# A scratch block in DRAM is turned around: the dense gates lie by group of four expert tiles, then partition, then block of 32 tokens

## The chip, the cores and the metric

The kernel runs on one core of a Trainium2 chip. The time is that of one execution on the device in microseconds (us). The kernel before took 4025.16 us, the median of three runs (4023.65 to 4027.57).

## The reference, cut to what matters

Two layers. Each has a mixer, and then a retrieval of experts ("PEER"): for every token, 8 heads pick 16 of 16,384 experts, each expert is one row of `U` and one of `V`, and the output is a gated sum.

```
q = (h @ w_q) per head and half;   s = q . subkeys
s_top, i_top = top_k(s, 16)                       # for both halves
best, pos = top_k(s_top[0] + s_top[1], 16)        # 16 of the 256 sums
idx = i_top[0][..] * 128 + i_top[1][..];  gate = softmax(best)
a   = einsum('td,thed->the', x, U[idx])
out = einsum('the,thed->td', gate * gelu(a), V[idx])
```

There are 544 tokens: 512 of a prompt and 32 of a sample group.

## The kernel before, in words

Of the 544 tokens the first 384 (`ND`) are computed densely: for every expert `a = gelu(x U^T)`, times a dense matrix of gates that is zero where an expert was not picked, times `V`. The other 160 tokens are done with gathered rows: indirect DMAs on POOL's queue fetch 128 rows of `U` or `V` at a time (tile `g_r`, four buffers), and DVE multiplies them out (`g_junk`, `g_acc`). The 16,384 experts are 128 tiles `j` of 128 partitions `i`; four tiles `j` are a group (`GA`), so there are 32 groups. The first 6 groups (`KEEP`) keep their activations in SBUF (tile `kept`), groups 6 to 17 write them to DRAM (`ad`, from tile `ga`, lines 934 and 941), and the rest are computed later, beside the dense sum.

The work of a layer around the change has two stages.

- **The gate stage.** For each of three blocks of 128 tokens, `second_stage` finds the picks and `make_g` builds the dense gates. For eight tokens at a time DVE writes one-hot matrices (`ohp`, `ohq`, `ohh`, `ohl`, lines 1360 to 1363), PE multiplies them (lines 1369 and 1370), and ACT copies the product into `stage` (line 1372), a tile of 128 partitions `i` by 128 tiles `j` by 32 tokens, in two buffers. After 32 tokens DVE multiplies the kept groups by their gates in place (line 1378), and ACT's queue writes the other 104 tiles `j` to the DRAM block `gd` (line 1379): 12 writes a layer, 24 in all. Expert activations (lines 95, 96, 115 and 934) and gathered rows are worked in between, by a budget of estimated times (`spend`).
- **The dense stage.** All 128 tiles `j` are taken in turn. For a group that isn't kept, SP's queue reads the group's gates from `gd` into `gt` (line 1079, two buffers), the activations `gr` come from `ad` or from `ga`, and DVE multiplies them (line 1092). Each is split into a high and a low part (`gwh` by ACT, `gwl` by DVE), `V` likewise (`vr` to `vh` and `vl`), and PE sums `gw^T v` for three blocks of tokens into PSUM (line 1113, 18 matmuls for a tile). The expert activations that are still missing (`wr` to `wh` and `wl`, then line 115) and the second half of the gathers run beside it.

The tiles of the dense stage (`gt`, `gwh`, `gwl`, `vr`) take the memory of the tiles of the gate stage (`stage`, the one-hot matrices). So the first to use such memory waits until the last reader of the old tile is done, and one of these readers is the last write of `gd`. The instructions of an engine run in the order in which they stand; a DMA queue takes its DMAs in the order in which they are issued, and a DMA's sixteen parts run on 16 DMA engines. In the profile, q1 is SP's queue, q10 ACT's, and q0 that of POOL's gathers.

Of the kernel before, what the change touches and what calls it, by code (L numbers as in the profile page):

```python
# [9 lines left out]
F32 = mybir.dt.float32  # L10
# [7 lines left out]
P = 128  # L18
# [17 lines left out]
NKEY = 128  # L36
# [8 lines left out]
ND = 384  # L45
# [3 lines left out]
ST = 32  # L49
TILE = (P, P, P, P, TS)  # L50
GA = 4
KEEP = 6
KJ = KEEP * GA
# [23 lines left out]
class Body:  # L77
# [881 lines left out]

    def peer(self, l):  # L960
        nc, a = self.nc, self.a
        gd = self.dp.tile([ND // ST, P, P, ST], F32, name=f"gd{l}")
        self.ad = self.dp.tile([P, NKEY // GA, GA, ND], F32, name=f"ad{l}")
        self.a_l, self.a_next, self.a_w = l, 0, None
        self.pre = {}
# [2 lines left out]
        with ExitStack() as es:  # L968
# [68 lines left out]
            with ExitStack() as es2:  # L1037
# [38 lines left out]
                for q in order:  # L1076
                    if q >= KEEP:
                        g4 = dn.tile([P, ND // ST, GA * ST], F32, name="gt", bufs=2)
                        nc.sync.dma_start(g4, gd[:, :, q * GA:(q + 1) * GA].rearrange("b i j t -> i b (j t)"))
                        if q < first // GA:  # L1080
                            ga4 = dn.tile([P, GA, ND], F32, name="gr", bufs=2)
                            nc.sync.dma_start(ga4, self.ad[:, q])
                        else:
                            ga4 = groups.pop(q)
                    for jj in range(GA):
                        j = q * GA + jj
# [33 lines left out]
                        if step % 4 == 0 and XAT <= step < XAT + 4 * (ND // P):  # L1120
                            i = (step - XAT) // 4
# [213 lines left out]
    def make_g(self, l, sp, gd, i, F):  # L1335

        nc = self.nc
        i1 = sp.tile([P, P], F16, name="i1T")
        i2 = sp.tile([P, P], F16, name="i2T")
        gh = sp.tile([P, P], F16, name="ghT")  # L1340
        gl = sp.tile([P, P], F16, name="glT")
        pr = self.bank(2)[:, :3 * P].rearrange("p (s t) -> p s t", s=3)
        for s in range(3):
            nc.tensor.transpose(pr[:, s], F[s].rearrange("p h k -> p (h k)"), self.ident)
        nc.scalar.copy(i1, pr[:, 0])
        nc.scalar.copy(i2, pr[:, 1])
        nc.scalar.activation(gh, pr[:, 2], AF.Copy, scale=GSCALE)
        nc.vector.scalar_tensor_tensor(gl, pr[:, 2], GSCALE, gh, op0=OP.mult, op1=OP.subtract)
        for c in range(0, P, OHT):
            if c % ST == 0:  # L1350
                stage = sp.tile([P, P, ST], F32, name="stage", bufs=2)

            sh = [P, OHT // 2, P, 2]

            def row(t):
                return t[:, c:c + OHT].rearrange("p (b t) -> p b t", t=2)[:, :, None, :].to_broadcast(sh)

            keys = self.io[:, None, :, :].to_broadcast(sh)
            p_, q_, qh, ql = (sp.tile(sh, F16, name=n, bufs=2) for n in ("ohp", "ohq", "ohh", "ohl"))
            nc.vector.tensor_tensor(p_, keys, row(i1), op=OP.is_equal)  # L1360
            nc.vector.tensor_tensor(q_, keys, row(i2), op=OP.is_equal)
            nc.vector.tensor_tensor(qh, q_, row(gh), op=OP.mult)
            nc.vector.tensor_tensor(ql, q_, row(gl), op=OP.mult)  # L1363
            self.spend(dve=2.45)
            for b in range(0, OHT, 4):
                ps = self.bank(2).rearrange("p (t j) -> p t j", t=4)
                for t in range(4):
                    w, half = (b + t) // 2, t % 2
                    nc.tensor.matmul(ps[:, t], p_[:, w, :, half], qh[:, w, :, half], start=True, stop=False)
                    nc.tensor.matmul(ps[:, t], p_[:, w, :, half], ql[:, w, :, half], start=False, stop=True)  # L1370
                o = (c + b) % ST
                nc.scalar.activation(stage[:, :, o:o + 4].rearrange("p j t -> p t j"), ps,  # L1372
                                     AF.Copy, scale=1.0 / GSCALE)
            self.t_pe += 0.9
            if (c + OHT) % ST == 0:
                t = i * P + c + OHT - ST
                k = self.kept[:, :, t:t + ST]
                nc.vector.tensor_mul(k, k, stage[:, :KJ])
                nc.scalar.dma_start(gd[t // ST, :, KJ:], stage[:, KJ:])

# [118 lines left out]
```

## Time and profile before

| | |
|---|---|
| median of three runs | 4025.16 us |
| the profiled execution's own time | 4027.84 us |
| its span | 4026.0 us |
| PE busy | 3878.3 us (96%) |
| DVE busy | 2950.2 us (73%) |
| ACT busy | 1603.4 us (40%) |
| POOL busy | 1038.8 us (26%) |
| granted clock of PE, mean | 0.978 |
| moved by DMA | 917.60 MB, mean 228 GB/s |

The profiled execution is 2.68 us longer than the median. Of its 4027.84 us, 1.84 us lie outside the span. The gate stage lies at about 980 to 1277 us in the first layer and 2960 to 3260 us in the second; the dense stage follows each. In the strips of 40 slices a slice is 100.65 us. Where a stage is judged, its own stretch of the trace is read, not the share over the span.

### The profile page before, as it was taken

What the parts mean: (1) busy time and instruction counts of PE and PEld (TensorE: products, weight loads), DVE (VectorE), ACT (ScalarE), POOL (GpSimd) and SP (SyncE); (2) the same over time, 40 slices, a digit from 0 to 9 for tenths busy, and PEclk for the clock granted to TensorE, in tenths of its full rate; (3) what the DMA queues carried; (4) which work ended last, traced back from release to release, by engine and by line L of the source; (5) the groups of instructions that cost most, each with busy time, mean ns of one, the idle gap of its engine ahead of it and who ended that gap; (6) DMA issues with size and microseconds to landing.
All of it is one profiled execution on the core that took longest, in us unless ns stands there. A gap on an engine that the chain in (4) does not pass through costs nothing.

```text
span 4026.0 us, 63148 instructions
## 1 busy us (share of the span) xinstructions
PE 3878.3 (96%) x24116; PEld 3522.3 (87%) x24116; DVE 2950.2 (73%) x5811; ACT 1603.4 (40%) x2373; POOL 1038.8 (26%) x880
## 2 busy tenths in 40 slices
PE   8999999999997999999999999999999889999998
PEld 7899997898996888888888999889989778888887
DVE  5544445789998888888855444467999978888887
ACT  4532333334554333333444333343355543333333
POOL 0110110003323444443401111000034434444443
PEclk9999999999997999999999999999999889999999
DMA  7233114427888999999933322162378899999996
GB/s 261 82 124 120 54 59 149 169 64 243 302 314 317 336 344 345 337 339 339 339 111 117 125 83 67 48 235 86 101 270 302 321 335 332 346 341 342 347 333 238
DMA packets 318272, 917.60 MB, mean 228 GB/s; under 512 B 28400, under 2 KB 109680, under 8 KB 314640
## 3 DMA queue, kind: packets, MB, share of 16 engines
q1 hardware_dynamic: 218896, 518.21, 38.0%
q0 software_dynamic: 92160, 335.59, 23.2%
q10 hardware_dynamic: 6912, 59.77, 3.7%
q8 instruction: 189, 3.10, 0.3%
q14 instruction: 115, 0.94, 0.1%
HBM read 826.19 MB, written 87.26 MB: 227 GB/s over the span
## 4 chain that ended last, share of the span: by engine, by line
PE 85%; DVE 8%; issue 3%; DMA 2%; ACT 2%; POOL 1%; DVEq 0%; POOLq 0%; SPq 0%; ACTq 0%
PE mm L115 31%; PE mm L1113 17%; PE sm L115 12%; PE sm L1113 9%; PE mm L341 2%; DVE wl L96 2%; DMA g_r<-u_rows,g_e 2%; DVE g_junk L1182 1%; PE sm L628 1%; PE sm L616 1%; PE sm L904 1%; PE sm L622 1%; PE sm L885 1%; DVE ohl L1363 1%; PE sm L522 1%
## 5 line engine op out<-in xcount | busy, mean ns | idle before, releaser
L95 ACT CAST wh<-wr 128x1024 fp32r<-128x1024 f32 (+1 forms) x464 | 466.9, 1006 | 1042.8 <-PE mm L115 676.0
L96 DVE TENSOR_TENSOR wl<-wr,wh 128x1024 fp32r<-128x1024 f32 (+1 forms) x464 | 543.3, 1171 | 384.2 <-ACT wh L95 383.5
L1197 POOL DMA_INDIRECT g_r<-u_rows,g_e x320 | 459.4, 1436 | 1374.3 <-DVE g_junk L1182 654.3
L1197 POOL DMA_INDIRECT g_r<-v,g_e x320 | 449.3, 1404 | 553.7 <-DVE g_acc L1190 511.1
L115 PE MATMUL mm<-ah,wh 128*128 128x384 f32 (+1 forms) x1408 | 467.5, 332 | 19.3 <-ACT ga L934 12.6
L115 PE MATMUL mm<-ah,wl 128*128 128x384 f32 (+1 forms) x1408 | 464.2, 332 | 15.0 <-DVE wl L96 14.7
L115 PE MATMUL mm<-al,wh 128*128 128x384 f32 (+1 forms) x1408 | 461.7, 328 | 0.5 <-DVE al L96 0.5
L1190 DVE SCALAR_TENSOR_TENSOR g_acc<-g_r,g_w,g_acc 128x1024 f32<-128x1024 f32 x320 | 409.7, 1280 | 12.3 <-DMA g_r<-v,g_e 10.3
L1182 DVE SCALAR_TENSOR_TENSOR g_junk<-g_r,h2t 128x1024 f16<-128x1024 f32 x320 | 390.0, 1219 | 30.3 <-DMA g_r<-u_rows,g_e 28.9
L96 DVE TENSOR_TENSOR vl<-vr,vh 128x1024 fp32r<-128x1024 f32 x256 | 312.3, 1221 | 38.7 <-ACT vh L95 38.3
L115 PE MATMUL mm<-hh,wh 128*128 128x272 f32 x1536 | 335.4, 295 | 0.2 <-ACT hh L95 0.2
L115 PE MATMUL mm<-hh,wl 128*128 128x272 f32 x1536 | 334.3, 295 | 0.0
L115 PE MATMUL mm<-hl,wh 128*128 128x272 f32 x1536 | 328.0, 293 | 0.0
L1113 PE MATMUL mm<-vl,gwh 128*128 128x512 f32 x1024 | 316.9, 390 | 0.0
L1113 PE MATMUL mm<-vh,gwl 128*128 128x512 f32 x1024 | 316.1, 390 | 0.0
L115 PE MATMUL sm<-ah,wl 128*128 128x384 f32 x896 | 303.5, 339 | 5.9 <-DVE wl L96 5.9
L1113 PE MATMUL mm<-vh,gwh 128*128 128x512 f32 x1024 | 304.1, 392 | 2.2 <-ACT vh L95 2.2
L115 PE MATMUL sm<-ah,wh 128*128 128x384 f32 x896 | 304.7, 340 | 0.7 <-ACT stage L1372 0.7
L115 PE MATMUL sm<-al,wh 128*128 128x384 f32 x896 | 303.6, 339 | 0.0
L115 PEld LDWEIGHTS mm<-ah,wh 128*128 128x128 f32 x1408 | 267.8, 190 | 28.2 <-ACT ga L934 18.8
L115 PEld LDWEIGHTS mm<-ah,wl 128*128 128x128 f32 x1408 | 267.6, 190 | 24.0 <-DVE wl L96 23.7
L95 ACT CAST vh<-vr 128x1024 fp32r<-128x1024 f32 x256 | 269.1, 1053 | 12.1 <-DMA vr<-v 11.4
(436 smaller groups left out, 8133.7 us busy)
## 6 DMA issues: line engine op xcount, KB each, us to landing
vr<-v SPq DMA_DIRECT2D x256, 512.0 KB, 6.9
wr<-u SPq DMA_DIRECT2D x240, 512.0 KB, 6.1
wr<-w_in SPq DMA_DIRECT2D x96, 512.0 KB, 3.6
gd<-stage ACTq DMA_DIRECT2D x24, 1664.0 KB, 8.5
gt<-gd SPq DMA_DIRECT2D x52, 768.0 KB, 10.7
ad<-ga ACTq DMA_DIRECT2D x24, 768.0 KB, 6.4
gr<-ad SPq DMA_DIRECT2D x24, 768.0 KB, 8.3
wr<-w_o SPq DMA_DIRECT2D x32, 512.0 KB, 3.8
```

The lines of the kernel that those rows point to most:

```text
L95: self.nc.scalar.copy(hi, src)
L96: self.nc.vector.tensor_sub(lo, src, hi.bitcast(F32))
L115: nc.tensor.matmul(o, w[:, k * P:(k + 1) * P], x[part][:, k], start=(q == 0), stop=(q == 3 * nk - 1))
L341: nc.tensor.matmul(ps[i][s][:np_], m[:, k, c], w[:, s * 512:(s + 1) * 512], start=(k == 0 and q == 0), stop=(k == NK - 1 and q == 2))
L522: nc.tensor.matmul(ps[i], x[:, k, i * P:(i + 1) * P], w[:, kk * BW:(kk + 1) * BW], start=(k == 0 and q == 0), stop=(k == NK - 1 and q == 2))
L616: nc.tensor.matmul(p[:, h], ats[:, h], dm[:, h], start=True, stop=True)
L622: nc.tensor.matmul(p[:, h], dtm[:, h], xm[:, h], start=True, stop=True)
L628: nc.tensor.matmul(p[:, h], xm[:, h], dtm[:, h], start=True, stop=True)
L1113: ins = nc.tensor.matmul(po[i][s], w[:, i * P:(i + 1) * P], v[:, s * 512:(s + 1) * 512], start=(step == 1 and m == 0), stop=(step == NKEY ...
L1182: ins = nc.vector.scalar_tensor_tensor(jk, r, 1.0, h2t[t], op0=OP.mult, op1=OP.mult, accum_out=w[:, s:s + 1])
L1190: nc.vector.scalar_tensor_tensor(acc[t], r, w[:, s:s + 1], acc[t], op0=OP.mult, op1=OP.add)
L1197: nc.gpsimd.indirect_dma_start(out=r, out_offset=None, in_=a["v" if which else "u_rows"].rearrange("l e d -> (l e) d"), in_offset=bass.Ind ...
```

## The change

The block `gd` of a layer had the axes block of 32 tokens, partition, tile `j`, token. Now it has group of four tiles, partition, block of 32 tokens, and then 128 elements (four tiles by 32 tokens). The bytes are the same, and so are the two DMA calls.

- The write (24 times, 1664 KB): a partition's 104 tiles by 32 tokens were one run of 13,312 bytes in DRAM, so the write was 128 runs. Now they are 26 runs of 512 bytes, 3328 runs in all. In SBUF they are contiguous in both.
- The read (52 times, 768 KB): a partition's gates of a group were 12 runs of 512 bytes, 1536 runs in all. Now they are one run of 6144 bytes, 128 runs in all.

```
-        gd = self.dp.tile([ND // ST, P, P, ST], F32, name=f"gd{l}")
+        gd = self.dp.tile([NKEY // GA, P, ND // ST, GA * ST], F32, name=f"gd{l}")
...
-                        nc.sync.dma_start(g4, gd[:, :, q * GA:(q + 1) * GA].rearrange("b i j t -> i b (j t)"))
+                        nc.sync.dma_start(g4, gd[q])
...
-                nc.scalar.dma_start(gd[t // ST, :, KJ:], stage[:, KJ:])
+                nc.scalar.dma_start(gd[KEEP:, :, t // ST].rearrange("q i j -> i q j"),
+                                    stage[:, KJ:].rearrange("p (q j) t -> p q (j t)", j=GA))
```

No instruction changes its place on any engine. These are the last rows of ACT's gate stage in the first layer, with the last write of `gd`:

```order
 L1372 ACTIVATE stage<-sm 128x4x128 x8
 L95 CAST wh<-wr 128x1024
-L1379 DMA gd_6639<-stage 128x3328
+L1379 DMA gd_6639<-stage 128x26x128
 L934 ACTIVATE ga<-sm 128x384
 L1187 ACTIVATE g_w_9072<-g_w_9072 128x16
```

The write stands between the same two instructions, and has 26 runs a partition in place of one. And this is SP's queue where the dense stage of the first layer begins:

```order
 L102 DMA wr<-u 128x1024 x32
 L1097 DMA vr<-v 128x1024 x3
-L1079 DMA gt<-gd_6639 128x12x128 x2
+L1079 DMA gt<-gd_6639 128x1536 x2
 L1082 DMA gr<-ad_6640 128x1536 x2
 L102 DMA wr<-u 128x1024 x3
```

Again only the shape differs: one run of 1536 elements a partition in place of 12 of 128.

## Rows read from the trace of the kernel before

**Rows 1.** The page: the DMA strip of 40 slices.
```profile
DMA  7233114427888999999933322162378899999996
```

**Rows 2.** Busy by stretch: length, PE, PEld, DVE, ACT, POOL, clock, DMA share, GB/s.
```profile
1000.00:1250.00 250.00, 224.12 (x1647) 210.84 (x1645) 248.47 (x377) 147.09 (x180) 79.40 (x54) 0.93 0.85 303
1300.00:1950.00 650.00, 648.90 (x3086) 565.34 (x3085) 535.74 (x648) 233.79 (x318) 280.56 (x206) 1.00 0.96 342
```

**Rows 3.** Waits of PE, 1290 to 2040 us: total us, times, longest.
```profile
PE mm L1113 <- ACT vh L95: 1.1, 1, 1.1
```

**Rows 4.** Chain of waits, 1150 to 1310 us: start, us, what.
```profile
1265.84 10.66 DMA gd<-stage
...
1277.70 14.33 PE sm L115 x72
```

**Rows 5.** Timeline of ACT, first layer: start, us, what, [idle before, releaser].
```profile
1232.20 0.33 ACTq L1379 DMA_DIRECT2D gd<-stage  x1
...
1247.28 0.33 ACTq L1379 DMA_DIRECT2D gd<-stage  x1
...
1265.84 0.33 ACTq L1379 DMA_DIRECT2D gd<-stage  x1
...
1276.92 0.51 ACT L95 CAST gwh<-kept 128x384 fp32r<-128x384 f32 x1 [5.85 <-DMA gd<-stage]
1277.34 1.04 ACT L95 CAST wh<-wr 128x1024 fp32r<-128x1024 f32 x1
...
1283.22 1.05 ACT L95 CAST wh<-wr 128x1024 fp32r<-128x1024 f32 x1 [4.45 <-PE sm L115]
```

**Rows 6.** Timeline of DVE, same place.
```profile
1275.27 1.23 DVE L1182 SCALAR_TENSOR_TENSOR g_junk<-g_r,h2t 128x1024 f16<-128x1024 f32 x1 [3.74 <-DMA g_r<-u_rows,g_e]
...
1280.09 1.22 DVE L96 TENSOR_TENSOR wl<-wr,wh 128x1024 fp32r<-128x1024 f32 x1
```

**Rows 7.** Timeline of ACT, second layer.
```profile
3248.53 0.33 ACTq L1379 DMA_DIRECT2D gd<-stage  x1
...
3259.89 0.52 ACT L95 CAST gwh<-kept 128x384 fp32r<-128x384 f32 x1 [5.21 <-DMA gd<-stage]
...
3263.81 1.05 ACT L95 CAST wh<-wr 128x1024 fp32r<-128x1024 f32 x1 [2.06 <-PE sm L115]
```

**Rows 8.** DMA queues, 1269.3 to 1276.3 us: packets, MB, share of 16 engines.
```profile
q10 hardware_dynamic: 141, 1.70, 57.4%
q0 software_dynamic: 209, 0.77, 29.2%
```

**Rows 9.** DMA queues, 1440.3 to 1443.9 us, a read of gd nearly alone.
```profile
DMA packets 1588, 0.95 MB, mean 264 GB/s; under 512 B 15, under 2 KB 1549, under 8 KB 1587
...
q1 hardware_dynamic: 1587, 0.94, 91.5%
```

**Rows 10.** DMA queues, 1427.8 to 1436.2 us, a read of gd beside gathers.
```profile
DMA packets 2193, 3.15 MB, mean 375 GB/s; under 512 B 80, under 2 KB 1615, under 8 KB 2193
...
q1 hardware_dynamic: 1683, 1.27, 48.5%
```

**Rows 11.** Busy by stretch, with PE's clock as third number from the end.
```profile
1275.00:1280.00 5.00, 2.30 (x9) 2.30 (x10) 4.37 (x6) 1.85 (x3) 1.68 (x1) 0.85 0.97 396
1280.00:1285.00 5.00, 5.00 (x25) 5.00 (x25) 3.15 (x6) 1.44 (x2) 2.62 (x2) 0.81 1.03 401
```

**Rows 12.** Waits of PE, 1264 to 1290 us and 3246 to 3270 us.
```profile
PE sm L115 <- DVE wl L96: 3.5, 2, 3.3
...
PE sm L115 <- DVE wl L96: 2.4, 1, 2.4
```

**Rows 13.** Tile gt: the issues on SP's queue, ns min/median/max.
```profile
L1079 SPq DMA_DIRECT2D gt<-gd x52: 377/377/11534, 1279.5 to 3938.2; - x52
```

**Rows 14.** Waits of DVE, 980 to 1290 us and 2960 to 3270 us.
```profile
DVE g_junk L1182 <- DMA g_r<-u_rows,g_e: 7.0, 5, 3.7
...
DVE g_junk L1182 <- DMA g_r<-u_rows,g_e: 8.7, 8, 3.0
```

## The prediction, made before the changed kernel was run

> **What bounds the kernel now.** I began with the strips of the page [rows 1]. That of DMA is at nine tenths in the dense stages, so a change that makes transfers there cheaper looks welcome. The busy time by stretch corrects this [rows 2]: in the dense stage PE is busy 648.90 of 650 us at a full clock, and DMA, at 0.96, is full beside it. The waits of PE over that stage show what DMA costs PE there [rows 3]: one wait of 1.1 us for a piece of `V`, and the second layer has a row that reads the same. So the 52 reads that become cheaper lie beside a busy PE. In the gate stage, where the 24 writes become dearer, DVE is the full engine (248.47 of 250 us), and ACT is busy 147.09 of 250.
>
> Between the two stages is the one place where `gd` itself is on the path. The chain of waits has it there [rows 4]: the last write is issued at 1265.84, takes 10.66 us, and PE's next long run starts at 1277.70. ACT's timeline shows how [rows 5]: it stands 5.85 us before the second `gwh`, which takes memory that the write still reads, and behind that wait, on the same engine, stands the cast `wh` on which an expert tile of PE depends. In the second layer the same wait is 5.21 us [rows 7].
>
> **What the reads give.** A read's 1536 packets become 128. They free DMA time in a stage where PE waits 1.1 us a layer. One thing may come of it: SP's issues of `gt` and of what stands behind them are held while a long read drains (the issues of `gt` run from 377 ns to 11,534 ns [rows 13]), and a late load of `V` is what PE's wait of 1.1 us ends on. I take that wait as gone: 2 x 1.1 = 2.2 us won. The rest is hidden by PE's own work; were PE not full there, some 26 us of DMA time a layer would count (26 reads by 1 us, below), but it is.
>
> **What a write costs.** In the 7.0 us in which the last write ran, its queue held the engines 57.4%, or 4.02 us, for 1.70 MB; gathers had 29.2%, and loads nearly all of the rest [rows 8]. The new write is 3328 packets of 512 bytes. No row shows such a write; the nearest is a read of `gd` that ran almost alone [rows 9]: 91.5% of 3.6 us, or 3.29 us, for 1549 small packets (0.79 MB) and some large ones (0.15 MB, 0.35 us at the rate of rows 8). That leaves 2.94 us x 16 engines / 1549 = 30 ns for a packet. 3328 x 30 ns / 16 = 6.3 us, in place of 4.02. (The same difference per byte makes a read cheaper by 2.9 - 1.9, so 1 us.)
>
> How long the write then lasts depends on its share. At 57.4% it is 6.3 / 0.574 = 11.0 us. Beside gathers, a read of small packets got 48.5% with the loads of its queue [rows 10]; at that, 13.0 us. From both sides: if 512 bytes cost no more per byte than 13,312, the window stays 7.0 us; if each packet lasts as it did beside gathers (8.4 us for 1615 packets, or 83 ns x 16 engines), it is 3328 x 83 / 16 = 17.3 us. I take 12 us, between the shares of rows 8 and 10: the write lands 5 us later, with bounds of 0 and 10.3 us.
>
> By the Trainium skill's "DMA: Bandwidth & Descriptors" (section "Why small descriptors are slow") each packet carries about 3 extra cycles beside one per 32 bytes. As an estimate that is 19 cycles for the 16 of 512 bytes, so 4.8 us for the write, and at 57.4% a landing 1.3 us later, which would leave nothing after the slack below. Rows 9 speak for more: 30 ns, against 19 ns (4.02 us x 16 / 3328) for the same bytes in long runs.
>
> **What of that is on the path.** First layer. The write lands at 1276.51 (rows 4: 1265.84 + 10.66), now at 1281.5. From the landing it takes 0.4 us until `gwh` starts, 0.42 to `wh`, 1.04 for it and 1.22 for `wl`, or 3.1 us if DVE is free; as it went, `wl` ended at 1281.31, 4.8 us after the landing, as other work stood before it [rows 6]. I take 3.9: PE can start that tile at 1285.4. Before, PE reached it only when the tile that it had begun at 1277.70 was done, about 1283.4 (`wh`'s buffer came free at 1283.22). So 2.0 us are lost.
>
> Second layer. The landing is 3259.89 - 0.4 = 3259.5 [rows 7]; PE reached that tile about 3264.0 (the buffer came free at 3263.81). Now 3264.5 + 3.9 = 3268.4, so 4.4 us are lost.
>
> The clock. In the first layer PE waited 3.5 us for `wl` [rows 12], and the granted clock then fell: 0.85 and 0.81 over two stretches of 5 us, 3.4 us at the lower of its two levels (1.2 GHz in place of 2.4), so 1.7 us of work lost [rows 11]. With a longer wait I expect such a dip again in the first layer, now behind the later tile, and a first one in the second (whose wait was 2.4 us): 2 x 1.7 = 3.4 us, since the dip of before lay under slack.
>
> PE's two waits of rows 12 came from `wl` standing on DVE behind a gathered row that was 3.74 us late [rows 6]. With small packets in ACT's queue I expect gathers to land sooner; but the next tile still waits for the write, so this moves idle time and wins none.
>
> The other 22 writes I cost at nothing. The cover is DVE's queue, which is full without them, and the second buffer of `stage`, filled again no sooner than the next write. In the last block of tokens they follow each other by 15 us (1232.20 and 1247.28 [rows 5]). A landing more than 15 us after the issue would hold ACT there; 12 us and the 3.5 us that lie between the last issue of rows 5 and the stretch of rows 8 would just reach it, but there fewer transfers stand before a write, so I leave it to the range.
>
> **The sum.** 2.0 + 4.4 + 3.4 - 2.2 = 7.6 us, and 1 us as an allowance for issues on ACT's queue that come to stand behind a long write: about 9 us. On the profiled execution (4027.84) that is 4036.8. It lies 2.7 us above the median of 4025.16, so I forecast 4034. About 0.2%, or 8 us, is what a measurement of this kernel can tell from no change. The forecast lies hardly beyond that bound.
>
> **Rivals.**
>
> - *The last write lands as early as now.* For it: 30 ns may be a read's price alone, and gathers that are served in the same 7 us could give way. The Trainium skill ("DMA: Bandwidth & Descriptors", "Specifications") names 512 bytes as the least for line rate, by which this would hold; the trace differs, with 264 GB/s for small packets nearly alone [rows 9] against 401 GB/s in the second stretch of [rows 11]. Then only the 2.2 us are won: 4023, no change.
> - *Faster.* Packets of 13,312 bytes no longer stand before the gathers, and if the write is not late, the waits of DVE for gathered rows in the gate stages go: 7.0 + 8.7 us [rows 14], on the engine that sets that stage's pace. With the 2.2 us that is 18 us: 4007. It decides only while the last write lands no more than about 1.5 us later than now; beyond that ACT's wait takes it back. Against it: most of these waits lie in the transition, behind the write.
> - *ACT is held, or small writes are slow.* 208 packets an engine is twice what a read of `gd` had, and such reads held SP up to 11.5 us [rows 13]. If each write holds ACT so that 3 us get through to DVE (about half of a hold of 6.3 us; ACT's idle 41% of rows 2 takes the rest), it is 24 x 3 = 72 us: 4097. If instead a small write lasts twice as long as a read, 60 ns, the transition alone gives 2 x (12.5 / 0.574 - 7.0) = 30 us, less 3 of slack: 4052.
>
> **Chances.** The forecast's own case, a landing 3 to 10 us later, has 0.62 and gives 4029 to 4046; a little more than half of it (0.35) lies over 8 us. The rival without a loss 0.14, faster 0.08, held or slow 0.16. So faster by over 0.2%: 0.08; within: 0.27 + 0.14 = 0.41; slower: 0.35 + 0.16 = 0.51. The range leaves out the faster rival and the far end of the slow one: 4019 to 4055.
>
> **What would show it.** In the changed kernel's trace: q10's 512-byte packets, with an own time near 6.3 us a write (4.0 would be the first rival, 12 the slow one); ACT's wait before the second `gwh`, 5.85 us and 5.21 us before, near 10 us; PE's gap before an expert tile there, with a dip of the clock in both layers; the issues of `gt` at most about 1 us. The dense stage after its first 30 us should take as long as before. The prediction is wrong if ACT's issues on line 1379 take microseconds, if DVE's busy share in the gate stage falls, or if ACT's wait stays near 6 us.

## The result, and the profile after

The changed kernel takes 4060.18 us (median of 4 runs, 4057.06 to 4066.54), and the kernel before, on the same chip, 4024.64 us (4 runs, 4023.65 to 4027.57). The ratio is 1.0085, with a 95% interval of 1.0071 to 1.0099: 35.5 us slower, outside the range of 4019 to 4055. The direction was forecast; the size was not.

The page of the changed kernel: the DMA strip of 40 slices (against rows 1), and below it packets and the two kinds of issues on `gd`, with KB and the median us from issue to landing (8.5 for the write and 10.7 for the read before).

```profile
span 4064.7 us, 63148 instructions
...
DMA  7233114417999899999933322171478989999996
...
DMA packets 321857, 917.60 MB, mean 226 GB/s; under 512 B 28401, under 2 KB 109681, under 8 KB 321297
...
gd<-stage ACTq DMA_DIRECT2D x24, 1664.0 KB, 11.4
gt<-gd SPq DMA_DIRECT2D x52, 768.0 KB, 7.9
```

The bytes are the same, the read lands sooner and the write later. Next the two stages of the first layer, each moved by as much as this execution is late there, 6 and 17.5 us (length, PE, PEld, DVE, ACT, POOL, clock, DMA share, GB/s).

```profile
1006.00:1256.00 250.00, 222.66 (x1641) 209.52 (x1640) 246.04 (x375) 144.68 (x179) 84.93 (x53) 0.93 0.91 301
1317.50:1967.50 650.00, 648.90 (x3085) 565.38 (x3084) 535.83 (x648) 233.53 (x318) 280.77 (x206) 1.00 0.92 336
```

Against [rows 2], PE is busy for the same 648.90 of 650 us in the dense stage, while DMA's share fell from 0.96 to 0.92. By the packets in the two traces a read of `gd` holds the engines 2.0 us in place of 2.9, or 23 us in the 26 reads of a layer, and nobody waited for those. So the reads are cheaper by about what was worked out, and hidden. In the gate stage DMA's share rose, from 0.85 to 0.91.

To see where time was lost I set each of DVE's 96 writes of the tile `ohp`, which run through both gate stages, beside the same one of before:

| place | before, us | after, us | late by |
|---|---|---|---|
| first `ohp`, layer 1 | 986.8 | 991.9 | 5.1 |
| last `ohp`, layer 1 | 1255.8 | 1263.2 | 7.4 |
| first `ohp`, layer 2 | 2967.5 | 2980.8 | 13.3 |
| last `ohp`, layer 2 | 3238.1 | 3263.9 | 25.8 |
| end of the span | 4026.0 | 4064.7 | 38.7 |

The 5.1 us at the top lie before any `gd` is written, and the profiles of all nine timed experiments below are late there by 4.9 to 6.6 us, two with the layout of before among them. So I don't count them as a cost of the change; the profile of before was early in that place. Of the rest, 2.3 us are lost in the first gate stage and 10.1 us at the first transition (DVE's instructions are late by 7.4 us ahead of it and by 17.5 behind it). 4.2 us of that are regained by the first `ohp` of the second layer. Then 12.5 us are lost inside the second gate stage, and 12.9 us from its last `ohp` on, which holds the second transition.

The transition first. ACT's timeline there (start, us, what, idle before and releaser), to be set beside [rows 5]:

```profile
1273.49 0.37 ACTq L1379 DMA_DIRECT2D gd<-stage  x1
...
1278.19 0.51 ACT L95 CAST gwh<-kept 128x384 fp32r<-128x384 f32 x1
1295.44 0.51 ACT L95 CAST gwh<-kept 128x384 fp32r<-128x384 f32 x1 [16.75 <-DMA gd<-stage]
1295.86 1.04 ACT L95 CAST wh<-wr 128x1024 fp32r<-128x1024 f32 x1
1296.81 0.48 ACT L934 ACTIVATE ga<-sm 128x384 f32<-128x384 f32 x1
```

The wait before the second `gwh` is the one of [rows 5], 5.85 us then and 16.75 now; the second layer's is 15.89 us in place of 5.21 [rows 7]. Behind it on ACT stand `wh` and `ga`, and PE waits for `ga`. PE's wait (total, times, longest; first layer, then second) was 3.5 and 2.4 us in [rows 12]:

```profile
PE sm L115 <- ACT ga L934: 11.4, 1, 11.4
```
```profile
PE sm L115 <- ACT ga L934: 11.2, 1, 11.2
```

Why the write landed late is read from the DMA queues between its first and its last packet (packets, MB, share of 16 engines), against [rows 8]: 18.7 us in place of 7.0.

```profile
DMA packets 4753, 6.82 MB, mean 365 GB/s; under 512 B 178, under 2 KB 3506, under 8 KB 4752
...
q1 hardware_dynamic: 720, 2.62, 34.4%
q0 software_dynamic: 688, 2.48, 32.5%
q10 hardware_dynamic: 3344, 1.70, 30.1%
```

The write's own time is 30.1% of 18.7, or 5.63 us (4.02 before). But gathers (q0) took 6.1 us and loads (q1) 6.4 in the same window, and the three together fill 97% of it. In the middle of the window the shares are these.

```profile
q0 software_dynamic: 366, 1.37, 55.6%
q1 hardware_dynamic: 228, 0.83, 33.9%
q10 hardware_dynamic: 512, 0.26, 14.4%
```

From 1283 to 1289 us, where all three queues had work throughout, the write had 14.4% of the engines, not the 57.4% of [rows 8]; in the 6 us ahead of that, when the loads had only begun, it still had 53.6%. The loads are there because SP was released earlier. SP's timeline, before and after:

```profile
1269.98 8.02 SPq L102 DMA_DIRECT2D wr<-u  x2
1278.05 1.38 SPq L1097 DMA_DIRECT2D vr<-v  x3
```
```profile
1277.67 4.01 SPq L102 DMA_DIRECT2D wr<-u  x2
1281.73 1.99 SPq L1097 DMA_DIRECT2D vr<-v  x3
1295.43 0.80 SPq L1079 DMA_DIRECT2D gt<-gd  x2
```

Before, the loads of `vr` were issued at 1278.05, 12.2 us after the write [rows 5] and behind its landing at 1276.5; now at 1281.73, 8.2 us after it and inside its window. They stand behind the second load of `wr`, which waits for a `wl` on DVE. Before, that `wl` stood behind the gathered row of [rows 6] that was 3.74 us late, and began 10.6 us after the write was issued; now that row is not late, and it begins 6.6 us after:

```profile
1276.42 1.22 DVE L96 TENSOR_TENSOR wl<-wr,wh 128x1024 fp32r<-128x1024 f32 x1
```
```profile
1280.10 1.22 DVE L96 TENSOR_TENSOR wl<-wr,wh 128x1024 fp32r<-128x1024 f32 x1
```

In the second layer it is the same: a wait of 3.05 us for such a row is gone, and `vr` is issued 8.8 us after the write in place of 11.7.

The loss inside the second gate stage is another one, and has two parts. DVE's waits there and at the transition behind it (total, times, longest):

```profile
DVE wl L96 <- ACT wh L95: 8.6, 3, 4.3
DVE g_junk L1182 <- DMA g_r<-u_rows,g_e: 8.5, 5, 5.4
```

The longest wait for a gathered row, 5.40 us at 3031.72, makes 5.4 of the 12.5 us. Such a late row is not shown to be the change's: gate stages with the layout of before have them as well (4.23 us in the run with long runs on both sides, 4.89 and 4.58 us in the kernel before with the tiles placed elsewhere). The other part, 7.1 us, comes where ACT is late with `wh`. The issues of `ad` on ACT's queue (ns min/median/max; 326/326/345 before), and ACT's timeline at one of them:

```profile
L941 ACTq DMA_DIRECT2D ad<-ga x24: 326/327/8474, 985.1 to 3220.4; - x24
```
```profile
3084.64 0.38 ACTq L1379 DMA_DIRECT2D gd<-stage  x1
...
3087.67 8.45 ACTq L941 DMA_DIRECT2D ad<-ga  x1
...
3096.24 1.04 ACT L95 CAST wh<-wr 128x1024 fp32r<-128x1024 f32 x1 [8.10 <-issue]
```

The write of `gd` itself is issued in 0.38 us. The next DMA on the same queue, 3 us behind it, holds ACT for 8.45 us, and `wh` for PE stands behind it. There are five such holds in this execution: 3.89 and 5.09 us in the first gate stage, 1.31, 8.45 and 8.47 in the second. By the packets in the trace, the five found 93 to 207 of the write's 208 packets an engine still to be served when they were issued; the nine other issues of `ad` behind a write that had not landed found 70 or fewer.

### The profile page after: what moved, and what is told of

Its sections match the earlier page's. It is cut to its first block, busy times and chain, and to the rows that moved or that the text cites. A ratio compares the mean times of both kernels' runs of the same rounds, so it can differ in the third digit from the quotient of the medians.

```text
span 4064.7 us, 63148 instructions
## 1 busy us (share of the span) xinstructions
PE 3886.8 (96%) x24116; PEld 3528.0 (87%) x24116; DVE 2949.9 (73%) x5811; ACT 1602.2 (39%) x2373; POOL 1063.8 (26%) x880
## 5 line engine op out<-in xcount | busy, mean ns | idle before, releaser
L1197 POOL DMA_INDIRECT g_r<-u_rows,g_e x320 | 488.3, 1526 | 1376.3 <-DVE g_junk L1182 662.2
L96 DVE TENSOR_TENSOR vl<-vr,vh 128x1024 fp32r<-128x1024 f32 x256 | 311.9, 1220 | 38.7 <-ACT vh L95 38.6
L95 ACT CAST vh<-vr 128x1024 fp32r<-128x1024 f32 x256 | 269.0, 1053 | 2.7 <-DMA vr<-v 2.7
## 6 DMA issues: line engine op xcount, KB each, us to landing
gd<-stage ACTq DMA_DIRECT2D x24, 1664.0 KB, 11.4
```

Of the source, the lines that this page charges most:

```text
L95: self.nc.scalar.copy(hi, src)
L96: self.nc.vector.tensor_sub(lo, src, hi.bitcast(F32))
L1197: nc.gpsimd.indirect_dma_start(out=r, out_offset=None, in_=a["v" if which else "u_rows"].rearrange("l e d -> (l e) d"), in_offset=bass.Ind ...
```

## The experiments

What they had to tell apart: whether the writes' short runs alone make the loss, or the reads have a part in it; whether it is ACT's wait for the last write, or the held issues; and why the last write's window is 18.7 us when its own time is 5.6. Windows below run from the first packet to the last of a layer's last write, and all ratios are to the kernel before on the same chip.

**Short runs on both sides.** The block lies by group, block of 32 tokens, partition: the write has 512-byte runs as in the changed kernel, the read has them as before.

```
-gd = self.dp.tile([NKEY // GA, P, ND // ST, GA * ST], ...)
+gd = self.dp.tile([NKEY // GA, ND // ST, P, GA * ST], ...)
-nc.sync.dma_start(g4, gd[q])
+nc.sync.dma_start(g4, gd[q].rearrange("b i x -> i b x"))
-nc.scalar.dma_start(gd[KEEP:, :, t // ST].rearrange("q i j -> i q j"), ...)
+nc.scalar.dma_start(gd[KEEP:, t // ST].rearrange("q i j -> i q j"), ...)
```

> Writes in runs of 512 bytes as in the changed kernel, reads in runs of 512 bytes as in the kernel before (the block lies by group, block of tokens, partition). Theory W (the short writes alone cost the time: the last write of a layer lands about 11 us later and holds ACT before the second gwh, and ACT's issues of ad are held behind a short write): 4058 to 4066 us, ACT's wait before the second gwh near 16 us in both layers, as after the change (16.7 and 15.9). Rival R (the long reads cost it, by what they let through earlier): near 4025 us.

Measured: 4062.89 us, ratio 1.0075 (1.0054 to 1.0095). Windows 19.0 and 18.2 us, issues of `ad` up to 8.6 us. The short writes alone make the whole loss.

**Long runs on both sides.** Layout and write of before, and the read takes 6144 bytes a partition in one run. It leaves out the right gates: what it reads lies elsewhere in the block.

```
-nc.sync.dma_start(g4, gd[:, :, q * GA:(q + 1) * GA].rearrange(...))
+flat = gd[q % (ND // ST), :, KJ:].rearrange("i j t -> i (j t)")
+nc.sync.dma_start(g4.rearrange("p b x -> p (b x)"), flat[:, o:o + ND * GA])
```

> Writes in long runs as in the kernel before, reads in runs of 6144 bytes (they read other gates than those of their group, so that part of the computation is changed; bytes and counts are the same). Theory W: the reads are hidden by PE, so 4020 to 4026 us, at most PE's two waits of 1.1 us won, and ACT's wait before the second gwh stays at 5 to 6 us. Rival R: 4050 us or more.

Measured: 4031.19 us, ratio 1.0002 (0.9990 to 1.0014), windows 6.6 and 7.4 us. Cheap reads win nothing that can be measured, and PE's waits for `vh` [rows 3] are still 1.1 us in each layer.

**Runs of 1024 bytes.** `gd` by groups of eight tiles; the read has runs of 512 bytes again.

```
-gd = self.dp.tile([NKEY // GA, P, ND // ST, GA * ST], ...)
+gd = self.dp.tile([NKEY // (2 * GA), P, ND // ST, 2 * GA * ST], ...)
...
```

> The block lies by groups of eight tiles: writes in runs of 1024 bytes (1664 packets in place of 3328), reads in runs of 512 bytes. Theory S (the DMA engines take packets from the queues in turn, so the share of the write goes with the size of its packets, and its lateness comes from the share, not from its own time): own time about 4.8 us, the last write's window between 7 and 18.6 us, near 12 us; time 4035 to 4050 us. Rival D (the number of runs alone, by the work to make them): ACT's held issues halve, but the landing follows the own time alone, 5 us against 5.6, so a window near 17 us and 4052 us or more.

Measured: 4055.53 us, ratio 1.0059 (1.0044 to 1.0074). Windows 17.6 and 16.5 us: not the 12 that half the packets were to give, but as the rival had it. The longest issue of `ad` is 5.4 us in place of 8.5. The queues over the first layer's window (17.5 us), and over 1283 to 1289 us:

```profile
q1 hardware_dynamic: 720, 2.62, 36.7%
q0 software_dynamic: 657, 2.37, 33.1%
q10 hardware_dynamic: 1676, 1.70, 28.1%
```
```profile
q0 software_dynamic: 349, 1.27, 51.7%
q1 hardware_dynamic: 263, 0.99, 40.3%
q10 hardware_dynamic: 240, 0.24, 11.2%
```

Half the packets of the write, and beside them the same 720 loads and nearly the same gathers. The window shrank by little because it is the sum of all three, not the write's time by a share.

**The gates' tiles in other memory.** The pools are cut so that `gwh` and `gwl` don't lie where `stage` was: ACT no longer waits for the last write. Layout and writes as in the changed kernel.

```
-dv, dn = self.pool("dv", es2), self.pool("dn", es2)
+d1, dn, d3 = self.pool("d1", es2), self.pool("dn", es2), self.pool("d3", es2)
+dv = d1
-wh = dn.tile([P, ND], F32R, name="gwh", bufs=2)
+wh = d1.tile([P, ND], F32R, name="gwh", bufs=2)
...
-vl = dv.tile([P, D], F32R, name="vl", bufs=2)
+vl = d3.tile([P, D], F32R, name="vl", bufs=2)
```

> The changed kernel, with the tiles of the dense stage in another order in SBUF: gwh and gwl no longer take memory that the last write of gd still reads; gt, which waits for that write anyway, and gr do. Theory P (the late landing costs time only through ACT's wait before the second gwh): ACT does not wait there, PE's gap of 11.7 us before an expert tile goes in both layers, and the time is 24 to 30 us below the changed kernel, 4030 to 4038 us. Rival Q (the landing is needed for gt soon after, so the wait only moves): PE waits about as long at the first tile of a group that is not kept, less than 8 us won, 4052 us or more.

Measured: 4040.13 us, ratio 1.0013 (1.0002 to 1.0024). The window is even longer, 23.5 and 23.8 us, and in the first layer PE has no wait behind it. ACT's timeline of the first layer:

```profile
1277.14 0.37 ACTq L1380 DMA_DIRECT2D gd<-stage  x1
...
1281.83 0.92 ACT L95 CAST gwh<-kept 128x384 fp32r<-128x384 f32 x2
...
1284.65 1.05 ACT L95 CAST wh<-wr 128x1024 fp32r<-128x1024 f32 x1 [1.90 <-PE sm L115]
```

Both `gwh` run together, 4.7 us behind the issue, and ACT then waits for PE and not for a DMA. From 1.0085 to 1.0013 is 0.72%, or 29 us: the larger part of the loss is that wait and what follows from it. The issues of `ad` are still held, up to 7.4 us.

**The same placement in the kernel before.**

> The kernel before, with the order of tiles in SBUF of the run e4 (gwh and gwl no longer in memory that the last write still reads). Theory P: ACT's wait of 5.85 and 5.21 us goes. PE's gaps there (3.6 and 2.7 us) came from a gathered row that was late, so most of them stays, and the tile behind is no longer late: 0 to 6 us won, a ratio of 0.9985 to 1.0. Rival: the wait had kept loads back from a full DMA, and without it gathers and the first vr come later: slower, 1.001 or more.

Measured, with the pools' edit above: 4031.49 us, ratio 1.0002 (0.9991 to 1.0013). So the waits of 5.85 and 5.21 us cost the kernel before nothing that can be measured, and the gain of the placement in the changed kernel is the change's loss given back, not a gain of its own.

**Loads behind the write.** The tiles are ordered so that `vr` waits for the last write, too; ACT still waits for it.

```
-dv, dn = self.pool("dv", es2), self.pool("dn", es2)
+dn, d0, d2, dv, d3 = (self.pool(n, es2) for n in ("dn", "d0", "d2", "dv", "d3"))
+d0.tile([P, 768], F32, name="pad")
...
```

> The changed kernel, with the tiles of the dense stage in another order in SBUF, so that SP's first load of V (vr) has to wait for the last write of gd, as the second gwh still does. Theory L (the last write is late because gathers and loads, issued earlier than before the change, are served in its window, some 6.2 us of each; own time 5.6 us): without the three loads of V the window falls from 18.6 and 17.9 us to 13 or 14, ACT's wait before gwh from 16.7 to about 12, and the time by 8 to 11 us against the changed kernel, a ratio to before of 1.0055 to 1.0068. Theory S (each queue has a fixed share by its packets, about 30% for the small ones): the window stays at 17 us or more, a ratio of 1.008 or more.

Measured: 4051.38 us, ratio 1.0055 (1.0038 to 1.0073); windows 15.1 and 13.6 us. ACT's wait, SP's issue of `vr`, and the queues over the window of the first layer:

```profile
1294.90 0.51 ACT L95 CAST gwh<-kept 128x384 fp32r<-128x384 f32 x1 [12.93 <-DMA gd<-stage]
```
```profile
1294.94 1.28 SPq L1098 DMA_DIRECT2D vr<-v  x3
```
```profile
q0 software_dynamic: 677, 2.44, 39.6%
q10 hardware_dynamic: 3344, 1.70, 37.4%
q1 hardware_dynamic: 288, 1.05, 17.0%
```

Loads fell from 6.4 to 2.6 us of DMA time, by 3.8, and the window from 18.7 to 15.1, by 3.6. In the second layer they fell by as much and the window by 4.3 us, from 17.9. So what was served beside the write is what lengthened it, about one for one.

**`ad` on SP's queue.** One line: `self.nc.sync.dma_start(self.ad[:, q], self.a_group)` in place of `nc.scalar`.

> The changed kernel, with the 24 writes of ad issued by SP in place of ACT, so that nothing stands behind a write of gd on ACT's queue. Theory H (ACT is held by an issue of ad for up to 8 us twice a layer, and that is what the gate stage lost): no issue on ACT over 0.6 us, the time from the first to the last one-hot instruction (ohp) back from 271.3 and 283.1 us to about 270 in both layers, and 5 to 12 us won: a ratio to before of 1.0055 to 1.0073. Rival C (ACT's slack covers the holds, and the gate stage's extra time is that of late gathers): no change, 1.008 or more.

Measured: 4055.12 us, ratio 1.0059 (1.0044 to 1.0075). No issue of `ad` is held, while ACT's wait at the transition stays (17.5 us in the first layer, and the second's below).

```profile
L941 SPq DMA_DIRECT2D ad<-ga x24: 326/327/338, 985.0 to 3214.5; - x24
```
```profile
ACT gwh L95 <- DMA gd<-stage: 14.5, 1, 14.5
```

The difference of ratios to the changed kernel is 0.26%, about 10 us; the two intervals (up to 1.0075, and from 1.0071) overlap a little. The gate stages were to come back to about 270 us each, from 271.3 and 283.1 (first to last `ohp`). The first takes 268.9; the second takes 275.6, and in it DVE waits 5.77 us for one gathered row. Whether the kernel before would gain by `ad` on SP's queue was not run.

**The last write in long runs.** The twelfth write of a layer goes to a block of its own, 13,312 bytes a partition in one run; the other eleven stay short. The read takes a second, small DMA.

```
+if t // ST == ND // ST - 1:
+    nc.scalar.dma_start(gdl[:, KJ:], stage[:, KJ:])
+    continue
...
+nc.sync.dma_start(g4[:, :nb], gd[q, :, :nb])
+nc.sync.dma_start(g4[:, nb], gdl[:, q * GA:(q + 1) * GA].rearrange("i j t -> i (j t)"))
```

> The changed kernel, but the last of the 12 writes of a layer goes in long runs to a block of its own (read back in runs of 512 bytes beside the other 11 blocks of tokens). Theory W2 (two thirds of the loss is this one write): ACT's wait before the second gwh back at 5 to 7 us, PE's gap there below 4 us, and 20 to 25 us won: a ratio to before of 1.002 to 1.0035; the issues of ad are held as in the changed kernel. Rival: the loss is spread over all 12 writes, and less than 8 us are won, 1.0065 or more.

Measured: 4040.41 us, ratio 1.0026 (1.0013 to 1.0039); windows 6.7 and 7.8 us, and ACT's wait as before the change:

```profile
1292.52 0.52 ACT L95 CAST gwh<-kept 128x384 fp32r<-128x384 f32 x1 [4.61 <-DMA gdl<-stage]
```

One write of twelve in each layer makes 0.59% of the 0.85%, or 24 us. What stays, 0.26%, fits the issues of `ad` that are still held (up to 8.0 us).

**Both cures.** The placement and `ad` on SP's queue, in the changed kernel.

> The changed kernel with both remedies: the order of tiles in SBUF of e4, and the writes of ad issued by SP as in e6. If the loss is made of the wait of ACT for the last write (e4 won 0.72%) and of ACT's held issues (e6 won 0.26%), both add up and the ratio to before is 0.9985 to 1.0005. If they overlap, or something else in the gate stage costs, 1.001 or more.

Measured: 4029.86 us (12 runs) against 4028.68 (17), ratio 1.0002 (0.9986 to 1.0017). No issue of `ad` is held, the gate stages take 268.9 us each from first to last `ohp` (269.0 and 270.6 before), and the windows of 22 to 23 us hurt nobody. So the two causes together are the whole loss, to within that interval. With both gone the changed kernel ties with the one before, and no version here is measurably faster than that.

**No gathers.** POOL fills the gathered rows with zeros in place of the gathers' DMAs, in the changed kernel and in the one before; this leaves the gathered rows out. One execution each.

> The changed kernel without the gathers' DMAs (the rows are set to zero by POOL, so that part of the result is left out). In the window of the last write only loads compete: theory L gives own 5.6 plus about 6.4 us of loads, a window of 11 to 13 us; a fixed share of 30% for the small packets would keep it near 18 us. Its time is not to be compared with the others.

> The kernel before without the gathers' DMAs, in the same way. DVE is not held by late rows, so SP's loads are issued during the last write, as after the change. If the engines take one packet from each queue in turn, a write of 8 packets of 13,312 bytes an engine lets only about 8 to 10 packets of loads through, 1.5 to 1.9 us: a window of 5.5 to 6.5 us. If what is issued first or smaller is simply served first, the loads' 6.4 us lie in the window here too, 9 us or more. Its time is not to be compared with the others.

Measured: 4024.69 us in the changed layout, 4015.74 in the one of before. This didn't do what it was made for: without gathers the last write is over before any load comes, so loads alone beside the write were not seen. It gives the write by itself, over 6.1 us and 4.2 us:

```profile
DMA packets 3351, 1.73 MB, mean 284 GB/s; under 512 B 16, under 2 KB 3344, under 8 KB 3351
...
q10 hardware_dynamic: 3344, 1.70, 91.6%
```
```profile
DMA packets 142, 1.70 MB, mean 406 GB/s; under 512 B 14, under 2 KB 14, under 8 KB 14
...
q10 hardware_dynamic: 142, 1.70, 96.4%
```

Alone, a short write lasts 1.9 us longer than a long one; in the kernel it was 11 to 12 us longer. The other 9 to 10 us are the queues beside it. Eleven issues of `ad` are held in the changed layout here too, for 1.2 to 3.7 us: the holds don't need gathers beside the write, but are shorter without them. The two times are 9.0 us apart, of which 4.9 lie ahead of the first `ohp`; with one execution each I draw nothing from that.

## Why the prediction was wrong

- **The reads.** Hidden, as said; issues of `gt` are at most 578 ns, as said [rows 13]. But the 2.2 us for PE's wait for `vh` [rows 3] didn't come: that wait reads 1.1 us in both layers of the changed kernel. It did not end on a late load that a held `gt` had delayed. What it ends on I did not find.
- **The write's own time.** Forecast 6.3 us, measured 5.63 in the window and 5.59 alone (91.6% of 6.1): 27 ns a packet, not the 30 of a read. So the first term was a little too high. The estimate of 4.8 us from the Trainium skill's "DMA: Bandwidth & Descriptors" (section "Why small descriptors are slow") was about as far off on the other side.
- **How long the write lasts: the step that failed.** "How long the write then lasts depends on its share" took the share between 57.4% and 48.5%, so 12 us, and bounded the landing at 10.3 us later. The write had 30.1%, and landed 21.6 us after its issue (1295.04, 0.4 before `gwh`, less 1273.49; 10.66 before), 10.9 us later: just past the far bound. Two things were wrong. The 57.4% is a share that a queue of 13,312-byte runs got, and does not pass over to one of 512-byte runs. And the 48.5% of [rows 10] is the share of all of q1, its large loads too: the 1615 small packets at the text's own 30 ns are 3.0 us of 8.4, or 36%, and 6.3 / 0.36 would have been 17.5 us. The nearest row was there; it was read wrongly. That 17.5 comes so near the 18.7 is in part luck, since no fixed share holds: with `vr` held back the write had 37.4%.
- **What was ready beside it.** "With small packets in ACT's queue I expect gathers to land sooner" was right at both transitions: DVE's waits for gathered rows in the first layer fell from 7.0 [rows 14] to 2.0 us, and in the second from 5.8 to 2.3 behind the last `ohp` (its total, 8.7 to 8.5, hides this behind the 5.40 us at 3031.72). But I stopped there. Rows that come sooner let DVE run sooner, free `wr`, and so release SP's loads into the write's window, where they take 6.4 us in place of 0.8. The timelines of DVE and SP show the release; the experiment with `vr` held back shows what the loads cost.
- **The path.** Right in mechanism: `gwh`, then what stands behind it on ACT, then PE. PE's gap grew by 7.9 us (11.4 for 3.5) and by 8.8 (11.2 for 2.4), where 2.0 and 4.4 were forecast from the smaller delay. PE resumed on `ga`, whose engine's queue was held by the same wait, and not on `wl`.
- **The clock.** A dip in both layers, as said. PE's clock in the first (third number from the end; 0.50 is the lower level), against [rows 11]:

```profile
1285.00:1290.00 5.00, 0.95 (x6) 0.63 (x4) 0.00 (x0) 0.00 (x0) 0.00 (x0) 0.97 1.04 417
1290.00:1295.00 5.00, 0.00 (x0) 0.00 (x0) 0.00 (x0) 0.00 (x0) 0.00 (x0) 0.50 0.77 285
1295.00:1300.00 5.00, 2.13 (x5) 1.62 (x6) 4.50 (x8) 3.17 (x5) 1.68 (x1) 0.50 0.72 252
1300.00:1305.00 5.00, 5.00 (x21) 5.00 (x21) 3.48 (x5) 0.00 (x0) 3.85 (x3) 0.66 1.00 416
```

  Idle time at the lower level costs nothing; 2.13 us of work at 0.50 and 5.00 at 0.66 cost 1.1 + 1.7 = 2.8 us, for the 1.7 a layer of the sum. That 1.7 counted idle time as work: PE was busy 2.30 and 5.00 us in the two stretches of [rows 11], so the dip of before cost 0.35 + 0.95 = 1.3 us by the same reckoning. With the gap's growth of 7.9 us that is 10.7 us if the dip of before lay under slack, as the text had it, and 9.4 if its 1.3 counts; DVE came out of the first transition 10.1 us later.
- **The other 22 writes.** Their landings cost nothing, as said, but not their place in ACT's queue. "1 us as an allowance for issues" was the second term that failed: 0.11% (with the wait already cured, 1.0013 to 1.0002, a difference that is not clear of the noise) to 0.26% (in the changed kernel), so 4 to 10 us. The single execution above fits the upper end: of the time lost in its gate stages, 2.3 and 7.1 us are not a late row. The length of a stage by itself doesn't tell the two apart: with the placement in the kernel before it took 279.1 and 275.4 us, where no issue was held but DVE waited for late rows. My sign for it, microseconds on the write's own issue, looked at the wrong instruction: the issue behind it waits. The other sign did show: DVE was busy 246.04 of 250 us in the first gate stage, where it had been 248.47 [rows 2].
- **The rivals.** "ACT is held, or small writes are slow" came nearest in time, with 4052 for its second half, but for another reason: a packet cost 27 ns, not 60, and the holds were five in 24 and not one for each write; that nearness is luck. *Faster*: at the transitions gathers did come sooner, and a write 10.9 us late took it back, as the rival's own condition said.

Of the loss of 0.85%, then, some 0.6 to 0.7% is shown to be ACT's wait for the last write, and 0.1 to 0.26% goes to the held issues, a share that the ratios give only roughly. Open is the rule by which a queue gets its share. The Trainium skill's "DMA: Bandwidth & Descriptors" (section "Queues, rings and completion order") says that a DMA engine takes turns between the queues that have work, and drains a packet of several descriptors from one before it goes on. That agrees in direction with the write's share of 14.4%, against 57.4% for long runs [rows 8], though there less stood beside the write. It doesn't explain the runs of 1024 bytes by itself: 240 of them were served in 6 us where 512 of 512 bytes were, so 0.24 and 0.26 MB, about the same bytes. No run here tells why. Open, too, is what makes a single gathered row come 4 to 6 us late in some executions.

## What to carry to other kernels

A transfer with short runs that shares the DMA engines with queues of long runs may end only when they have run dry: cost it by adding up all that can be ready in its window, its own time included, and ask what it will itself release into that window. Before making one side of a DRAM block contiguous, ask which side somebody waits for; here 52 reads were hidden, and two writes were not. And where memory is used again behind a transfer, another place for the tile that takes it can be worth more than the transfer's speed.

## What the runs showed of the hardware that was not expected

- A write with 512-byte runs alone moved 284 GB/s, one with 13,312-byte runs 406; a packet of the first costs 27 ns of an engine.
- Beside two busy queues the short write got 14.4% of the engines over 6 us, and 11.2% with runs of 1024 bytes.
- A DMA with 208 packets an engine is issued in 0.38 us, but the next DMA on that engine's queue, 3 us later, held its engine for 8.45 us; with runs of 1024 bytes the longest hold was 5.4, with 13,312 none (345 ns at most). In the changed kernel an issue was held when 93 or more of those 208 were left, and not when 70 or fewer were.
- Two profiles' gate stages can differ by 10 us through single gathered rows that come late: 268.9 us in both stages with both cures, where DVE waits at most 0.60 us for a row, and 279.1 with the placement in the kernel before, where it waits 4.89 and 4.58.
